# Attention by head pairs: logits on the two row halves, value sums feature-major on the two column halves

## The chip, the core and the metric

The kernel runs on one core of a Trainium2 chip. Time is device microseconds of one execution on that core. Its engines work through their own queues in order and meet at semaphores: PE multiplies matrices into PSUM (eight banks of 128 partitions x 512 floats), DVE and ACT do elementwise work and empty PSUM, POOL does some elementwise work, SP issues the loads.

## What is computed

The reference is two blocks of a network for 256 tokens of 1024 features: feed-forward halves, a Mamba-2 mixer, a sliding-window attention, a mixer of latent attention and RWKV-7, and a layer of experts. The change touches the sliding-window attention of the first block. It has 16 query heads of 64 features, two shared key/value heads (eight query heads each), a window of 128 tokens, a position bias and a sink for each head:

```python
q = rmsnorm((u @ w_q).reshape(bsz, t, ATT_KV_HEADS, ATT_GROUP, ATT_HEAD_DIM), q_norm)
s = jnp.einsum('bqkrd,bskd->bkrqs', qk, kk).astype(jnp.float32) * scale + bias
s = jnp.where(valid, s, -jnp.inf)
m = jnp.maximum(jnp.max(s, axis=-1, keepdims=True), sink)
p = jnp.exp(s - m)
denom = jnp.sum(p, axis=-1, keepdims=True) + jnp.exp(sink - m)
o = jnp.einsum('bkrqs,bskd->bqkrd', (p / denom).astype(vk.dtype), vk)
h = h + o.reshape(bsz, t, ATT_HEADS * ATT_HEAD_DIM) @ w_o
```

## The kernel before

Activations lie feature-major: `h` is 128 partitions x 8 groups of features x 256 tokens. Large products are made of three matmuls on a high and a low part of both operands (`mm3`, L151; `xhi`, `xlo`, `whi`, `wlo`). Weights come in loads of 512 KB (L127), are split by ACT (`whi`, L93) and DVE (`wlo`, L99), and each such piece feeds eight `mm3`, 24 matmuls of 256 columns.

`attention` (L651) is woven from generators: at each `yield` the next one writes its instructions, and what is written first stands first in each engine's queue. Three run in turn: `project(0)`, then `fill` with `project(1..3)` and the output projection, and `heads`. `project(m)` computes q for four heads (L672), copies it to `qT` (L673), squares it on POOL (L675), sums the squares with four matmuls of two columns (L682) and makes the scales `sc` on DVE (L688 to L691). `heads` starts one head at each step.

A head (`attn_head`, L611) takes these steps: logits, queries x keys, from 64 rows of `qT` and `kd` (even heads in the upper half, odd ones in the lower), in two matmuls for tokens 0 to 127 (128 keys) and 128 to 255 (256 keys), L617 and L618; scale and bias, the negated maximum, the bound by the sink on DVE (L621, L622, L624); the exponentials with their sums `den` on ACT (L627); three transposes on PE (L631); their copy `asT` by ACT (L636); the value sums with the transposed weights as the stationary operand and 64 value columns moving, tokens on the partitions, into the banks `po`, which eight heads share (L638 to L640). A float32 matmul stands in the trace as two records, one for each pass; a transpose, and a matmul of `mm3`, as one.

After eight heads `tail` (L708) adds the sink's exponential to `den`, takes the reciprocal, multiplies `po` by it into `otok` (L716), transposes that to feature-major on PE (L724) and splits it to `ohi` (ACT, L727) and `olo` (DVE, L728). Then `proj_half` (L252) of the output projection runs on these four groups of features; the second eight heads feed the second half. `attn_head` is also called by the latent attention of the second block, which stays as it is.

`bcast` (L196) spreads a column over partitions: the column, repeated, is the stationary operand and the identity moves.

Of the kernel before, what the change touches and what calls it, by code (L numbers as in the profile page):

```python
# [17 lines left out]
T = 256  # L18
# [5 lines left out]
def weave(gens, lag=1):  # L24

    live, t = [], 0
    gens = list(gens)
    while gens or live:
        if gens and t % lag == 0:
            live.append(gens.pop(0))  # L30
        for g in list(live):
            if next(g, live) is live:
                live.remove(g)
        t += 1
        yield
# [13 lines left out]
class Ctx:  # L49
# [146 lines left out]
    def bcast(self, rt, st, c, n, out):  # L196

        self.nc.tensor.matmul(out, rt[:, st, c:c + 1].to_broadcast([128, n]), self.ident, start=True, stop=True)
# [452 lines left out]
def attention(K, h, P, kv, w_q, w_o, bias, pool):  # L651
# [11 lines left out]
    otok = pool.tile([128, 2, 1024], F32, name="otok")  # L663
# [30 lines left out]
    def head(hd):  # L694
        kvh, p0, c = hd // 8, 64 * (hd % 2), (hd % 8) * 64
        while hd // 4 not in scaled:
            yield
        if hd % 8 == 0:
            po[kvh] = [K.bank("po") for _ in range(2)]
        s = pool.tile([128, 384], F32, name="as", tag="as", bufs=4)  # L700
        sT = pool.tile([128, 384], F32, name="asT", tag="asT", bufs=3)
        yield from attn_head(K, s, qT[p0:p0 + 64, hd // 2], kd[p0:p0 + 64, kvh], vtok[:, :, kvh * 64:kvh * 64 + 64],
                             sc[:, hd], (bias[:, hd, 128:256], bias[:, hd]), nsink[:, hd:hd + 1], nm[:, hd], den[:, hd],
                             [p[:, c:c + 64] for p in po[kvh]], sT, hd % 4 < 0)
        if hd % 8 == 7:
            tails.append(tail(kvh))

    def tail(g):  # L708
        gs = slice(8 * g, 8 * g + 8)
        V.tensor_tensor(u[:, gs], nm[:, gs], nsink[:, gs].unsqueeze(2).to_broadcast([128, 8, 2]), OP.subtract)  # L710
        A.activation(u[:, gs], u[:, gs], AF.Exp)
        yield
        V.tensor_add(den[:, gs], den[:, gs], u[:, gs])
        V.reciprocal(den[:, gs], den[:, gs])
        for st in range(2):
            V.tensor_tensor(otok[:, st, g * 512:(g + 1) * 512].rearrange("p (a b) -> p a b", b=64),  # L716
                            po[g][st].rearrange("p (a b) -> p a b", b=64),
                            den[:, gs, st].unsqueeze(2).to_broadcast([128, 8, 64]), OP.mult)
        for _ in range(1):
            yield  # L720
        for st in range(2):
            ps = K.bank()
            for i in range(4):
                TE.transpose(ps[:, i * 128:(i + 1) * 128], otok[:, st, (4 * g + i) * 128:(4 * g + i + 1) * 128], K.ident)  # L724
            dst = (slice(None), slice(g * 4, g * 4 + 4), slice(st * 128, st * 128 + 128))
            pr = ps.rearrange("p (a b) -> p a b", b=128)
            A.activation(ohi[dst], pr, AF.Copy)  # L727
            V.tensor_sub(olo[dst], pr, ohi[dst].bitcast(F32))  # L728
            yield
        done.append(g)  # L730

    def heads():
        for _ in weave((head(hd) for hd in range(16)), 1):
            if tails and next(tails[0], tails) is tails:
                tails.pop(0)
            yield
        while tails:
            if next(tails[0], tails) is tails:
                tails.pop(0)
            yield  # L740
# [10 lines left out]
    scaled, tails, done, po = [], [], [], {}  # L751
# [4 lines left out]
    run((p0, 1), (fill(), 1), (heads(), 1))  # L756
# [1213 lines left out]
```

## Time and profile before

| | us |
|---|---|
| median of 3 runs | 2186.6 (2182.05 to 2188.41) |
| profiled execution | 2188.62 |
| its span, first to last instruction | 2186.8 |
| PE busy | 2109.8 (96% of the span) |
| DVE busy | 1584.8 (72%) |
| ACT busy | 1055.1 (48%) |
| POOL busy | 407.1 (19%) |

The page gives for each engine how long it had an instruction at work. Since matmuls overlap, PE can be busy without being at its peak, and the same matmul takes about twice as long where the chip grants the engine its lower clock, 1.2 GHz, in place of 2.4; the granted clock stands in the tables by stretch of time, as a share of the higher one. The rows for the attention, at about 839 to 926 us of the span, follow behind the change.

### The profile page before, as it was taken

The numbers are of one execution on the slowest core, as the hardware profiler recorded it, in microseconds if no ns is written. First come the engines' busy times: TensorE is split into PE (matmuls) and PEld (weight loads), VectorE is DVE, ScalarE is ACT, GpSimd is POOL, SyncE is SP. The second block draws the span as 40 slices with busy tenths as digits, with TensorE's granted clock in tenths as the row PEclk, the third lists the DMA queues.
The fourth block names the chain that finished last, engine by engine and source line by source line (L and its number), as shares of the span: only waits on it lengthen the run. The fifth ranks groups of instructions, "written<-read, shape, count | busy, mean of one in ns | idle before, by whom it ended". The sixth has DMA issues, their size and how long they took to land. (4 is left out here: it accounts for less than half of the span.)

```text
span 2186.8 us, 40880 instructions
## 1 busy us (share of the span) xinstructions
PE 2109.8 (96%) x16474; PEld 1986.3 (91%) x16474; DVE 1584.8 (72%) x2857; ACT 1055.1 (48%) x1770; POOL 407.1 (19%) x310
## 2 busy tenths in 40 slices
PE   8999898899999999999998998999999999999999
PEld 8999887799999998899997878999999998888887
DVE  7665979766567656676659678998788887555655
ACT  5444467444444445454443345553444444454454
POOL 2003335700110021100144315762000000000000
PEclk9999999999999999799998899999999999999999
DMA  6555442377555553245542205542444444555554
GB/s 218 190 185 177 136 135 101 134 191 204 185 181 184 183 184 107 102 169 188 188 164 76 80 30 194 177 151 97 157 162 155 159 160 164 189 188 191 192 188 150
DMA packets 98280, 348.14 MB, mean 159 GB/s; under 512 B 11083, under 2 KB 13996, under 8 KB 97836
## 3 DMA queue, kind: packets, MB, share of 16 engines
q1 hardware_dynamic: 98092, 345.54, 46.6%
q8 instruction: 129, 2.11, 0.4%
q14 instruction: 59, 0.48, 0.1%
HBM read 344.05 MB, written 1.44 MB: 158 GB/s over the span
## 5 line engine op out<-in xcount | busy, mean ns | idle before, releaser
L99 DVE TENSOR_TENSOR wlo<-wraw,whi 128x1024 fp32r<-128x1024 f32 x561 | 701.7, 1252 | 293.9 <-ACT whi L93 292.0
L93 ACT ACTIVATE whi<-wraw 128x1024 fp32r<-128x1024 f32 x644 | 676.5, 1053 | 394.0 <-PE ps L155 198.8
L153 PE MATMUL ps<-xhi,wlo 128*128 128x256 f32 x1960 | 562.7, 287 | 20.4 <-DVE wlo L99 9.6
L154 PE MATMUL ps<-xlo,whi 128*128 128x256 f32 x1960 | 557.3, 284 | 3.2 <-DVE xlo L182 2.6
L155 PE MATMUL ps<-xhi,whi 128*128 128x256 f32 x1960 | 554.9, 283 | 0.0
L153 PEld LDWEIGHTS ps<-xhi,wlo 128*128 128x128 f32 x1960 | 376.2, 192 | 28.8 <-DVE wlo L99 8.6
L154 PEld LDWEIGHTS ps<-xlo,whi 128*128 128x128 f32 x1960 | 376.1, 192 | 5.8 <-DVE xlo L182 5.4
L155 PEld LDWEIGHTS ps<-xhi,whi 128*128 128x128 f32 x1960 | 375.5, 192 | 0.2
L153 PE MATMUL ps<-phi,wlo 128*128 128x256 f32 x1024 | 293.9, 288 | 11.3 <-DVE wlo L99 4.6
L154 PE MATMUL ps<-plo,whi 128*128 128x256 f32 x1024 | 288.1, 281 | 0.0
L155 PE MATMUL ps<-phi,whi 128*128 128x256 f32 x1024 | 287.2, 281 | 0.0
L99 POOL TENSOR_TENSOR wlo<-wraw,whi 128x1024 fp32r<-128x1024 f32 (+1 forms) x83 | 206.8, 2495 | 167.5 <-ACT whi L93 145.5
L153 PEld LDWEIGHTS ps<-phi,wlo 128*128 128x128 f32 x1024 | 193.8, 190 | 13.1 <-DVE wlo L99 5.3
L1676 PE MATMUL pacc<-whi,cl 128*128 128x512 f32 x512 | 203.6, 398 | 1.5 <-DVE cl L1668 1.5
L1678 PE MATMUL pacc<-whi,ch 128*128 128x512 f32 x512 | 200.5, 392 | 0.0
L1677 PE MATMUL pacc<-wlo,ch 128*128 128x512 f32 x512 | 199.2, 389 | 0.0
L153 PE MATMUL ps<-ghi,wlo 128*128 128x256 f32 x704 | 197.9, 281 | 0.0
L154 PE MATMUL ps<-glo,whi 128*128 128x256 f32 x704 | 197.6, 281 | 0.0
L155 PE MATMUL ps<-ghi,whi 128*128 128x256 f32 x704 | 197.5, 280 | 0.0
L154 PEld LDWEIGHTS ps<-plo,whi 128*128 128x128 f32 x1024 | 194.0, 189 | 0.0
L155 PEld LDWEIGHTS ps<-phi,whi 128*128 128x128 f32 x1024 | 193.3, 189 | 0.0
L154 PEld LDWEIGHTS ps<-glo,whi 128*128 128x128 f32 x704 | 132.6, 188 | 0.0
(534 smaller groups left out, 3371.3 us busy)
## 6 DMA issues: line engine op xcount, KB each, us to landing
wraw<-in_w SPq DMA_DIRECT2D x262, 512.0 KB, 3.7
wraw<-in_p_u SPq DMA_DIRECT2D x128, 512.0 KB, 3.6
wraw<-in_p_v SPq DMA_DIRECT2D x128, 512.0 KB, 3.6
wraw<-in_m_win SPq DMA_DIRECT2D x40, 512.0 KB, 3.7
wraw<-in_x_win SPq DMA_DIRECT2D x20, 512.0 KB, 3.6
wraw<-in_m_wout SPq DMA_DIRECT2D x16, 512.0 KB, 3.7
wraw<-in_p_wpq SPq DMA_DIRECT2D x16, 512.0 KB, 4.3
wraw<-in_a_wq SPq DMA_DIRECT2D x8, 512.0 KB, 3.5
```

The source lines that it names most:

```text
L93: nc.scalar.activation(hi, w, AF.Copy)
L99: (nc.vector if lo_eng == "dve" else nc.gpsimd).tensor_sub(lo, w, hi.bitcast(F32))
L153: nc.tensor.matmul(ps, wl, xh, start=first, stop=False)
L154: nc.tensor.matmul(ps, wh, xl, start=False, stop=False)
L155: nc.tensor.matmul(ps, wh, xh, start=False, stop=last)
L1676: TE.matmul(o, cl[:, t], vh[:, f], start=False, stop=False)
L1677: TE.matmul(o, ch[:, t], vl[:, f], start=False, stop=False)
L1678: TE.matmul(o, ch[:, t], vh[:, f], start=False, stop=last)
```

## The change

Heads are computed in pairs: `pair(n)` for heads 2n and 2n+1, eight pairs, a new one every second step, in place of 16 heads at one per step.

- The logits of both heads are written in turn, first the two 128-column matmuls, then the two of 256 columns; one head uses the upper 64 rows and the other the lower, each has its own bank. Ahead of them stands one `K.warm` matmul of 256 columns of zeros into the first of the two banks.
- Scale and bias stay one operation for each head and token half. The maximum is taken for both heads in one operation per token half, the bound by the sink in one for the pair.
- The sink's exponential, its addition to `den` and the reciprocal are done per pair, before the value sums, instead of once per eight heads.
- Of the copies of the transposes, ACT makes the first head's and DVE the second's.
- The value sums have the values (64 columns) as the stationary operand and the transposed weights moving, 256 and 128 columns. Their result is feature-major, one head in the upper 64 partitions of a bank and the other in the lower: on the two column halves.
- Since the tokens now lie along the free dimension, the reciprocals are spread over 64 partitions for each head and token half with `bcast`, four matmuls into the other half of the same bank. ACT copies them (`ao`), DVE multiplies by the value sums, and ACT and DVE split the product into `ohi` and `olo`.
- `otok`, its 16 transposes and `tail` are gone. The first half of the output projection may start after four pairs.

```diff
     def bcast(self, rt, st, c, n, out):
 
-        self.nc.tensor.matmul(out, rt[:, st, c:c + 1].to_broadcast([128, n]), self.ident, start=True, stop=True)
+        r = rt if st is None else rt[:, st]
+        self.nc.tensor.matmul(out, r[:, c:c + 1].to_broadcast([128, n]), self.ident, start=True, stop=True)
...
+    def pair(n):
+
+        kvh, gs, halves = n // 4, slice(2 * n, 2 * n + 2), (slice(0, 64), slice(64, 128))
+        while n // 2 not in scaled:
+            yield
+        s = pool.tile([128, 2, 384], F32, name="as", tag="as", bufs=3)
+        sT = pool.tile([128, 2, 384], F32, name="asT", tag="asT", bufs=2)
+        pl = [K.bank() for _ in range(2)]
+        K.warm(pl[0], 1)
+        for e, p in enumerate(halves):
+            TE.matmul(pl[e][:, 0:128], qT[p, n, 0:128], kd[p, kvh, 0:128], start=True, stop=True)
+        for e, p in enumerate(halves):
+            TE.matmul(pl[e][:, 128:384], qT[p, n, 128:256], kd[p, kvh], start=True, stop=True)
+        yield
+        for e in range(2):
+            hd = 2 * n + e
+            for st, (a, b) in enumerate(SPANS):
+                V.scalar_tensor_tensor(s[:, e, a:b], pl[e][:, a:b], sc[:, hd, st:st + 1], bias[:, hd, 128 - 128 * st:], OP.mult, OP.add)
+        for st, (a, b) in enumerate(SPANS):
+            V.tensor_reduce(nm[:, gs, st], s[:, :, a:b], AX.X, OP.max, negate=True)
+        V.tensor_tensor(nm[:, gs], nm[:, gs], nsink[:, gs].unsqueeze(2).to_broadcast([128, 2, 2]), OP.min)
+        yield
+        for e in range(2):
+            hd = 2 * n + e
+            for st, (a, b) in enumerate(SPANS):
+                A.activation(s[:, e, a:b], s[:, e, a:b], AF.Exp, bias=nm[:, hd, st:st + 1], accum_out=den[:, hd, st:st + 1])
+        V.tensor_tensor(u[:, gs], nm[:, gs], nsink[:, gs].unsqueeze(2).to_broadcast([128, 2, 2]), OP.subtract)
         A.activation(u[:, gs], u[:, gs], AF.Exp)
         yield
+        pt = [K.bank() for _ in range(2)]
+        for e in range(2):
+            for b in range(3):
+                TE.transpose(pt[e][:, b * 128:(b + 1) * 128], s[:, e, b * 128:(b + 1) * 128], K.ident)
         V.tensor_add(den[:, gs], den[:, gs], u[:, gs])
         V.reciprocal(den[:, gs], den[:, gs])
+        yield
+        A.activation(sT[:, 0], pt[0][:, :384], AF.Copy)
+        V.tensor_copy(sT[:, 1], pt[1][:, :384])
+        yield
+        po = K.bank()
+        v = vtok[:, :, kvh * 64:kvh * 64 + 64]
+        for e, p in enumerate(halves):
+            TE.matmul(po[p, 0:256], v[:, 0], sT[:, e, 0:256], start=True, stop=False)
+        for e, p in enumerate(halves):
+            TE.matmul(po[p, 128:256], v[:, 1], sT[:, e, 256:384], start=False, stop=True)
         for st in range(2):
...
+            for e, p in enumerate(halves):
+                K.bcast(den[:, 2 * n + e], None, st, 64, po[p, 256 + st * 128:384 + st * 128])
+        yield
+        o = pool.tile([128, T], F32, name="ao", tag="ao", bufs=2)
+        A.activation(o, po[:, 256:512], AF.Copy)
+        V.tensor_tensor(o, o, po[:, 0:256], OP.mult)
+        yield
+        A.activation(ohi[:, n], o, AF.Copy)
+        V.tensor_sub(olo[:, n], o, ohi[:, n].bitcast(F32))
+        if n % 4 == 3:
+            done.append(n // 4)
...
-    run((p0, 1), (fill(), 1), (heads(), 1))
+    run((p0, 1), (fill(), 1), (weave((pair(n) for n in range(8)), 2), 1))
```

PE's queue behind the last matmul of the q projection (`mm3` on `xhi`), before:

```order
L155 MATMUL ps<-xhi,whi 128x256
L638 MATMUL po<-vtok,asT 128x64
L639 MATMUL po<-vtok,asT 128x64
L640 MATMUL po<-vtok,asT 128x64
L631 MATMUL ps<-cst,as 128x128 x3
L617 MATMUL ps<-kd,qT 128x128
L618 MATMUL ps<-kd,qT 128x256
L638 MATMUL po<-vtok,asT 128x64
```

The same place in the changed kernel (L736 and L738 are the value sums, L199 the spreading, L726 the transposes, L77 the `K.warm` matmul, L704 and L706 the logits):

```order
L155 MATMUL ps<-xhi,whi 128x256
L736 MATMUL ps<-asT,vtok 64x256 x2
L738 MATMUL ps<-asT,vtok 64x128 x2
L199 MATMUL ps<-cst,den 64x128 x4
L726 MATMUL ps<-cst,as 128x128 x6
L77 LDWEIGHTS zero
L77 MATMUL ps<-zero 128x256
L704 MATMUL ps<-kd,qT 128x128 x2
L706 MATMUL ps<-kd,qT 128x256 x2
L682 MATMUL ps<-cst,qsq 128x2 x4
```

One group now serves two heads. From here to the first matmul on `ohi` the queue holds nine value sums, eight heads' transposes, seven heads' logits, eight transposes of `otok` and one group L682 before, and three pairs' value sums, three pairs' transposes, two pairs' logits and one group L682 after.

PE's queue where the output projection begins, before, and then in the changed kernel:

```order
L724 MATMUL ps<-cst,otok 128x128 x4
L638 MATMUL po<-vtok,asT 128x64
L639 MATMUL po<-vtok,asT 128x64
L640 MATMUL po<-vtok,asT 128x64
L631 MATMUL ps<-cst,as 128x128 x3
L153 MATMUL ps<-ohi,wlo 128x256
```

```order
L736 MATMUL ps<-asT,vtok 64x256
L726 MATMUL ps<-cst,as 128x128 x3
L736 MATMUL ps<-asT,vtok 64x256
L738 MATMUL ps<-asT,vtok 64x128 x2
L199 MATMUL ps<-cst,den 64x128 x4
L726 MATMUL ps<-cst,as 128x128 x3
L153 MATMUL ps<-ohi,wlo 128x256
```

Before, the value sums of 13 heads stand ahead of the first matmul on `ohi`; after, those of five pairs. The other pairs' groups stand between the pieces of the output projection, and 120 of its 192 matmuls behind the last of them (108 before).

DVE's queue in the same stretch, before (L728 makes `olo` of the first eight heads):

```order
L621 SCALAR_TENSOR_TENSOR as<-ps,qsc,t5b 128x128
L621 SCALAR_TENSOR_TENSOR as<-ps,qsc,t5b 128x256
L622 TENSOR_REDUCE nm<-as 128x1 x2
L621 SCALAR_TENSOR_TENSOR as<-ps,qsc,t5b 128x128
L624 TENSOR_SCALAR nm<-nm,nsink 128x2
L622 TENSOR_REDUCE nm<-as 128x1
L621 SCALAR_TENSOR_TENSOR as<-ps,qsc,t5b 128x256
L728 TENSOR_TENSOR olo<-ps,ohi 128x4x128
```

and in the changed kernel (L711 scale and bias and L713, L714 the maximum of pair 4, L745 the product of pair 2, L731 the copy of pair 3's second head):

```order
L711 SCALAR_TENSOR_TENSOR as<-ps,qsc,t5b 128x128
L711 SCALAR_TENSOR_TENSOR as<-ps,qsc,t5b 128x256
L711 SCALAR_TENSOR_TENSOR as<-ps,qsc,t5b 128x128
L711 SCALAR_TENSOR_TENSOR as<-ps,qsc,t5b 128x256
L713 TENSOR_REDUCE nm<-as 128x2 x2
L745 TENSOR_TENSOR ao<-ao,ps 128x256
L714 TENSOR_TENSOR nm<-nm,nsink 128x4
L731 COPY asT<-ps 128x384
L720 TENSOR_TENSOR qu<-nm,nsink 128x4
L748 TENSOR_TENSOR olo<-ao,ohi 128x256
```

The copy for which a pair's value sums on PE wait stands behind the logits of the next pair and the product of the one before.

## Rows read from the trace of the kernel before

**Rows 1.** Busy time by engine in stretches cut where the granted clock changes.

```profile
core 0: us, PE busy (x) PEld busy (x) DVE busy (x) ACT busy (x) POOL busy (x), PEclk, DMA share, GB/s
...
844.10:847.60 3.50, 3.50 (x19) 3.28 (x17) 3.50 (x16) 1.35 (x6) 0.00 (x0) 0.51 0.01 2
...
857.80:864.60 6.80, 6.80 (x30) 5.86 (x29) 2.98 (x12) 2.24 (x9) 0.00 (x0) 0.50 0.15 53
...
874.60:902.20 27.60, 27.17 (x107) 21.81 (x108) 12.93 (x47) 9.85 (x36) 0.00 (x0) 0.51 0.06 19
...
sum 87.10, PE 86.38 PEld 76.11 DVE 54.81 ACT 41.69 POOL 9.50; mean PE 12.34 PEld 10.87 DVE 7.83 ACT 5.96 POOL 1.36
```

**Rows 2.** Instructions on `ohi`: count, ns, first and last start.

```profile
L155 PE MATMUL ps<-ohi,whi x64: 276/281/415, 900.1 to 926.4; 128*128 128x256 f32 x64
```

**Rows 3.** Timeline of PE, full clock: start, length, instructions, count.

```profile
870.26 0.50 PE L631 MATMUL ps<-cst,as 128*128 128x128 f32 x3
870.68 0.49 PE L617 MATMUL ps<-kd,qT 64*128 64x128 f32 x2
...
871.53 0.43 PE L638 MATMUL po<-vtok,asT 128*128 128x64 f32 x2
...
872.25 0.50 PE L631 MATMUL ps<-cst,as 128*128 128x128 f32 x3
...
873.53 1.05 PE L682 MATMUL ps<-cst,qsq 128*128 128x2 f32 x8
```

**Rows 4.** Timeline of PE, one head at the lower clock.

```profile
881.41 0.69 PE L638 MATMUL po<-vtok,asT 128*128 128x64 f32 x2
...
885.10 0.69 PE L638 MATMUL po<-vtok,asT 128*128 128x64 f32 x2
```

**Rows 5.** Timeline of PE, long matmuls at the full clock.

```profile
902.82 0.28 PE L153 MATMUL ps<-ohi,wlo 128*128 128x256 f32 x1
902.94 0.28 PE L154 MATMUL ps<-olo,whi 128*128 128x256 f32 x1
```

**Rows 6.** Timeline of PE, the first heads' logits.

```profile
839.34 0.50 PE L617 MATMUL ps<-kd,qT 64*128 64x128 f32 x4
839.66 0.61 PE L618 MATMUL ps<-kd,qT 64*128 64x256 f32 x4
840.10 0.38 PE L617 MATMUL ps<-kd,qT 64*128 64x128 f32 x2
...
841.21 1.05 PE L682 MATMUL ps<-cst,qsq 128*128 128x2 f32 x8 [0.30 <-POOL qsq L675]
```

**Rows 7.** Timeline of PE, two heads' sums in the mamba stage.

```profile
317.37 0.66 PE L490 MATMUL ps<-sc,xtok 128*64 128x256 f32 x4
317.85 0.40 PE L491 MATMUL ps<-sc,xtok 128*64 128x128 f32 x4
318.17 0.50 PE L473 MATMUL ps<-ahl,identr 64*128 64x256 f32 x2
```

**Rows 8.** Timeline of DVE, logits and maxima.

```profile
842.06 0.73 DVE L621 SCALAR_TENSOR_TENSOR as<-ps,qsc,t5b 128x256 f32<-128x256 f32 x2
842.71 0.60 DVE L622 TENSOR_REDUCE nm<-as 128x1 f32<-128x256 f32 x2
843.23 0.22 DVE L624 TENSOR_SCALAR nm<-nm,nsink 128x2 f32<-128x2 f32 x1
```

**Rows 9.** Groups by line, 826 to 927 us: count, busy us, mean ns.

```profile
L99 DVE TENSOR_TENSOR wlo<-wraw,whi 128x1024 fp32r<-128x1024 f32 x16 | 19.7, 1230 | 8.1 <-ACT whi L93 8.1
...
L636 ACT ACTIVATE asT<-ps 128x384 f32<-128x384 f32 x16 | 7.6, 491 | 20.8 <-PE ps L631 19.3 <-PE po L640 1.4
...
L716 DVE TENSOR_TENSOR otok<-po,den 128x512 f32<-128x512 f32 x4 | 2.6, 683 | 0.0
...
L171 DVE SCALAR_TENSOR_TENSOR rsq32t<-rsq32a,rsq32t 128x8 f32<-128x8 f32 x4 | 0.6, 156 | 0.0
```

**Rows 10.** Waits, 826 to 927 us: total us, times, longest.

```profile
DVE TC L792 <- DMA px<-in_xcols: 0.3, 1, 0.3
```

More of the change, by code (lines that the diff above doesn't have):

```diff
@@ L662, in attention @@
     u = pool.tile([128, 16, 2], F32, name="qu")
-    otok = pool.tile([128, 2, 1024], F32, name="otok")
     ohi = pool.tile([128, 8, T], F32R, name="ohi")
@@ L692, in project @@
         scaled.append(m)
-    def head(hd):
-        kvh, p0, c = hd // 8, 64 * (hd % 2), (hd % 8) * 64
-        while hd // 4 not in scaled:
+    def pair(n):
+        kvh, gs, halves = n // 4, slice(2 * n, 2 * n + 2), (slice(0, 64), slice(64, 128))
+        while n // 2 not in scaled:
             yield
[L698 to L706, printed above, removed]
@@ L708, in tail @@
-    def tail(g):
-        gs = slice(8 * g, 8 * g + 8)
-        V.tensor_tensor(u[:, gs], nm[:, gs], nsink[:, gs].unsqueeze(2).to_broadcast([128, 8, 2]), OP.subtract)
+        s = pool.tile([128, 2, 384], F32, name="as", tag="as", bufs=3)
[4 more added lines that the diff above has]
+            TE.matmul(pl[e][:, 0:128], qT[p, n, 0:128], kd[p, kvh, 0:128], start=True, stop=True)
@@ L712, in tail @@
         yield
+        pt = [K.bank() for _ in range(2)]
+        for e in range(2):
+            for b in range(3):
+                TE.transpose(pt[e][:, b * 128:(b + 1) * 128], s[:, e, b * 128:(b + 1) * 128], K.ident)
         V.tensor_add(den[:, gs], den[:, gs], u[:, gs])
         V.reciprocal(den[:, gs], den[:, gs])
-        for st in range(2):
-            V.tensor_tensor(otok[:, st, g * 512:(g + 1) * 512].rearrange("p (a b) -> p a b", b=64),
-                            po[g][st].rearrange("p (a b) -> p a b", b=64),
-                            den[:, gs, st].unsqueeze(2).to_broadcast([128, 8, 64]), OP.mult)
@@ L719, in tail @@
[L719 to L740, printed above, removed]
+        yield
[4 more added lines that the diff above has]
+        v = vtok[:, :, kvh * 64:kvh * 64 + 64]
@@ L749, in fill @@
             yield from K.proj_half(blk, g, ohi[:, 4 * g:4 * g + 4], olo[:, 4 * g:4 * g + 4], h)
-    scaled, tails, done, po = [], [], [], {}
+    scaled, done = [], []
     p0 = project(0)
```

## The prediction, written before the changed kernel ran

> **What bounds the kernel now.** I read the page first: PE has work in nearly the whole span, DVE and ACT in far less of it, so a stage is worth what PE spends in it. The change touches the attention alone, so I then read its stretch, from the first logit matmul to the last matmul on `ohi` at 926.4 us [rows 1, 2]: 87.1 us, of which PE is busy 86.38, DVE 54.81 and ACT 41.69. The windows are cut where the granted clock changes: it is at its lower level (1.2 of 2.4 GHz) in 3.5, 6.8 and 27.6 us, together 37.9 us [rows 1]. Before a fall PE ran heads and narrow `L682` matmuls (at 841.21 and at 873.53 us [rows 3, 6]), and before each rise the long matmuls of a projection. The third stretch has no such matmuls until the output projection begins, and there DVE is busy only 12.93 of 27.6 us. PE sets the pace, at the lower clock.
>
> One head costs PE 1.99 us at the full clock, from one group of transposes to the next: 0.42 for them, 0.85 for the logits, 0.72 for the value sums [rows 3]. At the lower clock it costs 3.69 us [rows 4], 1.85 times as much. So the 37.9 us would be 20.5 at the full clock: the low clock costs 17.4 us. A check: 288 long matmuls (96 of the q projection after the first logits, 192 of the output projection) at 0.12 us [rows 5] are 34.6, three groups `L682` at 1.0 [rows 6] are 3.0, 16 heads are 31.8, and 16 transposes of `otok` at about 0.11 are 1.8; with the 17.4 that makes 88.6, against 87.1 measured.
>
> **The change, part by part: PE.** All at the full clock, for one pair. Logits: the first two heads of before already lie on the two row halves one behind the other, and their eight passes (x4 and x4) take from 839.34 to 840.10, 0.76 us [rows 6], where one head alone takes 0.85. So two heads side by side are shown, and I take 0.9 with the change of mode. Six transposes with the change of mode: 0.84. The filler matmul `K.warm`: one of 256 columns, 0.12. Value sums: the mamba stage has the same pattern (two heads, 64 columns each, 256 and then 128 moving columns, on two column halves of one bank), and it takes from 317.37 to 318.17, 0.80 us [rows 7], against 1.44 for two heads now. The reciprocals' spreading is new: four matmuls of 128 columns on the same halves, as two steps like the `L491` step of 0.32, with one drain less: 0.55, between 0.4 and 0.65. Sum 3.2 us per pair, 25.7 for eight. Now it is 31.8 + 1.8 = 33.6. **PE: -7.9 us.**
>
> **DVE and ACT.** Two logit operations follow each other by 0.65 us for one head, its two maxima by 0.52 [rows 8]. Per pair: 1.3 for the four logit operations, 0.95 for two wider maxima with the same elements, about 0.6 for four small ones, 0.5 for the copy of the second head's transposes (ACT's copy of 384 columns takes 0.491 [rows 9]), and 0.75 for product and difference of 256 columns, which are half of the 0.683 row [rows 9] each and some fixed time. That is 4.1 us. PE needs only 3.2. While projections run between the heads this is covered, because a piece of 24 long matmuls costs PE 2.8 us [rows 5] and DVE one split of weights, 1.23 [rows 9]. Between the last matmul of the q projection and the first of the output projection it is not. By the order PE has there three value sums, three groups of transposes, two of logits and one `L682`, about 3 x 3.2 + 1.0 = 10.6 us; DVE has 3 x 4.1, two splits of weights at 1.23 and 13 small steps for the scales at about 0.16 [rows 9], 16.9 us. The value sums of a pair wait for the copy `L731`, and before it stand four logit operations, two maxima and the product of other pairs; behind it stand the next pair's logits, for which ACT waits, and then the transposes. The difference is 6.3 us if DVE comes in without a lead, and 0 if it is a whole pair ahead. DVE has some lead, since nothing holds it in the projections. **New waits: +5 us**, from 0 to 7.
>
> Here a rule of the Trainium skill speaks against the change. TensorEngine Tiling (Array Packing), Performance Considerations, PSUM Bottleneck, says that tiling speeds up TensorE but not the emptying of PSUM, which may become the bottleneck. This trace agrees in the sums: the pair falls on PE, and rises on DVE. If it held in the whole stretch, it would be the first rival below.
>
> ACT exchanges like for like: its exponentials stay, one copy of `asT` per pair moves to DVE, a copy of the spread sums and smaller pieces of `ohi` come in. The exponential of the sink now stands once per pair instead of once per eight heads, and waits for DVE; behind it is the split of weights, `whi`, which the output projection needs 24 matmuls later. ACT is busy in under half of the stretch [rows 1], and I cost it at nothing; without that cover it would be some 0.2 us per pair, like a small step on DVE. The GpSimd work is the same. On SP the load of `px` goes one weight load later. DVE waits 0.3 us for it now [rows 10]; the last 120 matmuls of the output projection, 14 us of PE, lie over a wait of one or two microseconds.
>
> **The clock.** The three places with an `L682` stay, and after each I expect a fall. What differs is how soon long matmuls follow: before, nine value sums, eight groups of transposes and seven of logits stand between the projections; now three, three and two. I take the first two falls as they are, 3.5 and 6.8 us [rows 1], and for the third the 10.6 us of PE less what passes before the fall, with waits: about 9. So 19.3 us at the lower clock, and as each costs 0.46 of its time, 8.9 us in place of 17.4. **Clock: -8.5 us**, from 0 (as long as now) to -17.4 (no fall at all).
>
> **Sum:** -7.9 + 5 - 8.5 = -11.4 us. The profiled execution took 2188.62 us with a span of 2186.8, so 1.8 lie around it and stay: 2177.2 for one like it. It stands 2.0 above the median of the runs, 2186.6, so against the median I say **2175 us**.
>
> **Rivals.**
> DVE sets the pace and the clock stays low as long as now: -7.9 + 6.3 + 0, 2185 us. For it speaks that the waits thin out PE's work exactly where the clock falls now. Against it: long matmuls come earlier, and each of the first two low stretches ended within about one piece of them [rows 1]. Chance 0.20.
> The clock hardly falls: side by side two heads fill more of PE's time, and with the filler matmul only one short fall remains: -7.9 + 4 - 14, 2169 us. For it: the mamba stage's pairs. Against it: `L682` leaves PE thin whatever the heads do. Chance 0.17.
> Slower: the waits for DVE bring the clock down early, and pieces of 24 long matmuls between heads no longer bring it back, until the last 120. Of 48 us of PE work before those (25.7 + 3.0 + 168 x 0.12) about 70% would be at the lower clock, 34 x 0.85 = 29 us of cost against 17.4 now; -7.9 + 5 + 11.6 is +8.7, 2195 us. The time is longer than before once more than 44 us run at the lower clock (0.46 x 44 is the 17.4 of now and the 2.9 left of the gain). Against it: the rises at 847.6 and 864.6 [rows 1], each after one piece of 24. Chance 0.08.
> The halves do not run side by side here: logits, value sums and spreading cost up to twice, +1.7 us a pair, +13.6 in all: -11.4 + 13.6, 2189 us. Rows 6 and 7 speak against it [rows 6, 7]. Chance 0.02.
>
> **How the numbers follow.** The forecast has 0.53, with its own range of -4 to -17 us (2169.5 to 2182.5), from waits of 0 to 7 and clock costs of 5 to 14. Of the cases, a change of over 0.3% (6.6 us, about what a measurement of this kernel can tell from none) faster holds 0.47 of the forecast, all of the second rival and 0.03 of the first: 0.67. Slower by that much: 0.09, the third rival and a tail of the fourth. Within: 0.24. The range for 8 in 10 goes from 2166 (second rival with fewer waits) to 2187 (first rival and a little).
>
> **What would show it.** In the changed trace: the two heads' logit matmuls start within hundredths of a microsecond of each other, and a pair's group takes about 0.9 us; value sums and spreading about 1.35. PE's waits should be on DVE's copy `L731` and on ACT's exponentials, 5 us in all, and lie after the last q projection. The windows at the lower clock should sum to 15 to 23 us, the output projection should begin 10 to 15 us earlier than at 899.7, and the last 120 matmuls should run unbroken. I would be wrong if the low clock still lasts over 30 us, if PE waits over 8 us for DVE, or if time changes outside 839 to 927 us by more than 2 or 3 us (the granted clock could fall elsewhere as stages shift).

## The result and the profile after

The changed kernel takes 2166.2 us (median of 12 executions) where the kernel before took 2187.9 beside it: a ratio of 0.991, 95% interval 0.989 to 0.9931, about 20 us less (21.7 between the medians). The direction was as forecast; the size was not, since the sum gave 11.4 us. The one of the twelve that was profiled ran at a granted clock of 0.555 from end to end (3338.5 us), so the rows below are from another execution.

> The changed kernel as it is, for a profile at the usual clock. The measured gain is about 20 us where 11.4 were forecast (-7.9 PE work, +5 waits for DVE, -8.5 clock). Theory: PE's work fell as forecast, but the stretch at the lower clock is shorter than the 19 us forecast, 5 us or less, and the waits for DVE are under 5 us. Rival 1: the clock falls as forecast, about 19 us, and the waits are absent. Rival 2: the attention gains only some 11 us, and the rest comes from other stages, whose spans shift by 5 us or more.

That one took 2160.96 us, beside 2183.33 for the kernel before. The kernel before was profiled once more as well, to see how regular its low clock is.

> The kernel before once more, for a second profile of it. Theory: the fall of the clock in its attention is regular, 30 to 40 us at the lower level, 85 to 88 us from the first logits to the last matmul of the output projection. Rival: it differs from execution to execution, under 25 us here, and then part of the 17.4 us that I put on the low clock belongs to the one execution that was profiled.

It took 2191.68 us. The first theory held for this execution: 37.5 us at the lower level in 87.3 us of attention, in three stretches as before [rows 1]. It does not hold for all. Of the 80 executions of the kernel before that stand beside the runs below, ten took 2169.9 to 2174.4 us at a mean granted clock of 0.978 to 0.982, and the other 70 took 2179.0 to 2199.5 us at 0.966 to 0.979; both profiles are of the larger group. So one profile in which the clock stays up does not by itself show that an edit holds it, and the clocks of all executions of a kernel are named below where it matters. Busy time by engine in stretches of time, the kernel before again (columns as in rows 1):

```profile
core 0: us, PE busy (x) PEld busy (x) DVE busy (x) ACT busy (x) POOL busy (x), PEclk, DMA share, GB/s
...
847.30:850.70 3.40, 3.40 (x17) 3.20 (x16) 3.40 (x16) 1.30 (x6) 0.00 (x0) 0.50 0.01 2
860.90:867.70 6.80, 6.80 (x29) 5.85 (x28) 2.98 (x12) 2.24 (x9) 0.00 (x0) 0.50 0.14 53
878.00:905.30 27.30, 26.87 (x106) 21.52 (x105) 12.69 (x46) 9.60 (x34) 0.00 (x0) 0.50 0.06 20
842.50:929.80 87.30, 86.58 (x539) 76.34 (x539) 55.03 (x162) 41.94 (x108) 9.75 (x10) 0.78 0.25 90
```

The same view of the changed kernel, cut at the start of the output projection, answers rows 1 and 2:

```profile
843.20:875.80 32.60, 32.60 (x298) 27.14 (x298) 30.98 (x113) 24.17 (x77) 3.12 (x3) 1.00 0.24 82
875.80:907.00 31.20, 30.11 (x265) 27.83 (x264) 26.27 (x58) 17.55 (x41) 6.54 (x7) 1.00 0.48 164
843.20:907.00 63.80, 62.71 (x561) 54.97 (x561) 57.25 (x171) 41.71 (x117) 9.66 (x10) 1.00 0.36 123
```

The attention takes 63.8 us instead of 87.3, and PEclk reads 1.00: in this execution the clock doesn't fall in it at all. PE is busy for all but 1.1 us, and its waits there come to one line (total us, times, longest):

```profile
PE ps L726 <- ACT as L719: 1.1, 2, 0.9
```

The rest of the execution took 2160.96 - 63.8 = 2097.2 us; it was 2101.5 in the first profile of before and 2104.4 in the second. In the profiles of the experiments below that leave those stages as they are it lies between 2097.0 and 2104.4. So some 7 us outside the attention differ from execution to execution of the same code, and what is said below of parts of the change goes by the attention's own stretch, with the medians beside it.

One pair on PE at the full clock, which answers rows 3 and 6 (start, length, instructions, count):

```profile
870.25 0.65 PE L736 MATMUL ps<-asT,vtok 128*64 128x256 f32 x4
870.74 0.39 PE L738 MATMUL ps<-asT,vtok 128*64 128x128 f32 x4
870.95 0.61 PE L199 MATMUL ps<-cst,den 128*64 128x128 f32 x8
871.49 0.87 PE L726 MATMUL ps<-cst,as 128*128 128x128 f32 x6
872.20 0.27 PE L77 MATMUL ps<-zero 128*128 128x256 bf16 x1
872.40 0.49 PE L704 MATMUL ps<-kd,qT 64*128 64x128 f32 x4
872.73 0.60 PE L706 MATMUL ps<-kd,qT 64*128 64x256 f32 x4
873.26 0.43 PE L736 MATMUL ps<-asT,vtok 128*64 128x256 f32 x1
```

From start to start: value sums 0.70, spreading 0.54, transposes 0.71, filler 0.20, logits 0.86, together 3.01 us for two heads.

### The profile page after: what moved, and what is told of

Read it like the earlier page. It is cut to its first block, busy times and chain, and to the rows that moved or that the text cites. A ratio compares the mean times of both kernels' runs of the same rounds, so it can differ in the third digit from the quotient of the medians.

```text
span 3336.8 us, 40935 instructions
## 1 busy us (share of the span) xinstructions
PE 3312.4 (99%) x16498; PEld 2977.1 (89%) x16498; DVE 1574.6 (47%) x2867; ACT 1067.6 (32%) x1780; POOL 395.1 (12%) x310
## 4 chain that ended last, share of the span: by engine, by line
PE 99%; DVE 1%; ACT 0%; issue 0%; DMA 0%; SPq 0%; DVEq 0%; ACTq 0%
PE ps L153 23%; PE ps L155 23%; PE ps L154 23%; PE pacc L1688 6%; PE pacc L1686 6%; PE pacc L1687 6%; PE ps L1633 2%; PE wo L153 1%; PE wo L155 1%; PE wo L154 1%; PE ps L199 1%; PE ps L491 0%; PE ps L1557 0%; PE ps L726 0%; PE ps L77 0%; PE ps L190 0%
## 5 line engine op out<-in xcount | busy, mean ns | idle before, releaser
L153 PE MATMUL ps<-xhi,wlo 128*128 128x256 f32 x1960 | 750.6, 383 | 7.3 <-DVE wlo L124 7.2
L154 PE MATMUL ps<-xlo,whi 128*128 128x256 f32 x1960 | 747.1, 381 | 0.4 <-DVE xlo L182 0.2
L155 PE MATMUL ps<-xhi,whi 128*128 128x256 f32 x1960 | 747.1, 381 | 0.0
L153 PEld LDWEIGHTS ps<-xhi,wlo 128*128 128x128 f32 x1960 | 574.2, 293 | 15.0 <-DVE wlo L124 7.4
L155 PEld LDWEIGHTS ps<-xhi,whi 128*128 128x128 f32 x1960 | 578.2, 295 | 0.8 <-issue 0.2
L154 PEld LDWEIGHTS ps<-xlo,whi 128*128 128x128 f32 x1960 | 576.5, 294 | 1.7 <-DVE xlo L182 1.2
L153 PE MATMUL ps<-phi,wlo 128*128 128x256 f32 x1024 | 395.5, 387 | 2.4 <-ACT phi L1507 2.4
L155 PE MATMUL ps<-phi,whi 128*128 128x256 f32 x1024 | 392.4, 383 | 0.0
L154 PE MATMUL ps<-plo,whi 128*128 128x256 f32 x1024 | 390.6, 381 | 0.9 <-DVE plo L1508 0.9
L155 PEld LDWEIGHTS ps<-phi,whi 128*128 128x128 f32 x1024 | 294.6, 288 | 0.0
L155 PE MATMUL ps<-ghi,whi 128*128 128x256 f32 x704 | 269.8, 383 | 0.0
L155 PEld LDWEIGHTS ps<-ghi,whi 128*128 128x128 f32 x704 | 208.3, 296 | 0.0
```

The costliest lines, as they stand in the source:

```text
L153: nc.tensor.matmul(ps, wl, xh, start=first, stop=False)
L154: nc.tensor.matmul(ps, wh, xl, start=False, stop=False)
L155: nc.tensor.matmul(ps, wh, xh, start=False, stop=last)
```

## The experiments: which part keeps the clock up

The largest difference to the forecast is the clock, so four kernels take the change apart. The kernel without the filler:

```diff
-        K.warm(pl[0], 1)
```

> The changed kernel without the filler matmul ahead of each pair's logits; all else is as changed. What is asked of the four runs of this call: which part of the change keeps the granted clock at its full level in the attention (0 us at the lower level there, against 37.9 before). Theory, sums: the new form of the value sums does it (64 stationary columns and 256 or 128 moving ones, where 128 stationary ones met 64 moving). Then the clock stays up without the filler, under 4 us at the lower level in the attention, and the time is the changed kernel's less eight fillers at about 0.12 us: 0 to 1 us below it, some 20 to 22 us below before. Rival, filler: the filler does it; then 15 to 30 us at the lower level come back, which cost 7 to 14 us, and the kernel is only 8 to 14 us below before.

Measured 2162.05 us, ratio to before 0.990 (0.9867 to 0.9933), the same as the changed kernel within the interval. Its attention by engine (here and below the columns are those of rows 1, and rows at a PEclk of about 0.50 are all that fell):

```profile
843.90:907.20 63.30, 61.92 (x555) 54.44 (x555) 57.15 (x172) 41.84 (x117) 9.61 (x10) 1.00 0.36 123
```

The clock stays up without the filler, with a mean over the whole execution of 0.978 to 0.985 in all eight, and the attention is 0.5 us shorter: the theory held. The filler alone, in the kernel before (logits of every second head):

```diff
     ps = K.bank()
+    K.warm(ps, fillers)
     TE.matmul(ps[:, 0:128], q[:, 0:128], k[:, 0:128], start=True, stop=True)
```

> The kernel before with nothing added but eight fillers in the attention, one ahead of the logits of every second head. Theory, sums: the clock falls as before, 30 to 40 us at the lower level between the first logits and the end of the output projection, and the time is before's plus about 1 us (8 x 0.12). Rival, filler: the low level there shrinks to under 10 us, which gives back 13 to 17 us of the 17.4 that it costs, and the time is 12 to 16 us below before.

Measured 2182.6, ratio 0.9989 (0.9958 to 1.002).

```profile
859.60:869.80 10.20, 10.20 (x45) 9.22 (x45) 4.78 (x22) 2.72 (x10) 0.00 (x0) 0.50 0.03 8
844.60:922.40 77.80, 76.66 (x546) 67.31 (x546) 54.71 (x161) 41.74 (x108) 9.63 (x10) 0.93 0.29 101
```

Neither theory has this right. In the profiled execution, with eight fillers, 10.2 us are at the lower level instead of 37.5, and the attention takes 77.8 us. The medians show only 4 us of these 9.5, the interval reaches to no change at all, and the ten executions go from 2168.6 us at a mean clock of 0.983 to 2191.0 at 0.972. So how much the fillers hold by themselves is not shown. The first part of the change with the filler, but the old value sums and tails:

```diff
-        po = K.bank()
-        for e, p in enumerate(halves):
-            TE.matmul(po[p, 0:256], v[:, 0], sT[:, e, 0:256], start=True, stop=False)
+        for e in range(2):
+            TE.matmul(p0, sT[:, e, 0:128], v[:, 0], start=True, stop=True)
+            TE.matmul(p1, sT[:, e, 128:256], v[:, 0], start=True, stop=False)
+            TE.matmul(p1, sT[:, e, 256:384], v[:, 1], start=False, stop=True)
```

> The first part of the change and the filler alone: logits of two heads in turn on the two row halves, by pairs, but value sums token by token with 64 moving columns, the division and the 16 transposes per eight heads as before. Theory, sums: the clock still falls, 20 to 38 us at the lower level, since the old value sums are there; PE saves 8 x (2 x 0.85 - 0.9) = 6.4 us on the logits and pays 1 for fillers, so 4 to 12 us below before (12 if the low stretches get shorter by a third). Rival, logits or filler: the clock stays up, under 8 us at the lower level, and the time is 19 to 23 us below before (6.4 - 1 and 14 to 17 of clock).

Measured 2169.4, ratio 0.993 (0.9898 to 0.9961).

```profile
858.80:862.20 3.40, 3.40 (x18) 3.40 (x18) 2.34 (x9) 1.38 (x6) 0.00 (x0) 0.50 0.22 67
882.70:889.50 6.80, 4.95 (x22) 4.56 (x23) 4.28 (x12) 3.90 (x16) 0.00 (x0) 0.50 0.00 0
843.60:914.90 71.30, 68.24 (x545) 63.39 (x545) 56.45 (x145) 38.48 (x100) 9.69 (x10) 0.93 0.31 110
```

As in the profile with the filler alone, 10.2 us remain at the lower level. That is between the two theories, and so is the time, 17 us below before; 1.85 us of the second stretch are PE's own idle time. The second part alone, heads one by one and no filler:

```diff
-    TE.matmul(o[0], sT[:, 0:128], v[:, 0], start=True, stop=True)
+        for e, p in enumerate(halves):
+            TE.matmul(po[p, 0:256], v[:, 0], sT[:, e, 0:256], start=True, stop=False)
+        for e, p in enumerate(halves):
+            TE.matmul(po[p, 128:256], v[:, 1], sT[:, e, 256:384], start=False, stop=True)
+        yield
+        for st in range(2):
+            for e, p in enumerate(halves):
+                K.bcast(den[:, 2 * n + e], None, st, 64, po[p, 256 + st * 128:384 + st * 128])
```

> The second part alone: logits of one head after the other as before, no filler, but value sums feature-major on the two column halves with the reciprocals spread, once per two heads. Theory, sums: the clock stays up, under 8 us at the lower level in the attention. PE pays 1.35 us per pair for sums and spreading where 1.44 stood, and the 16 transposes (1.8 us) go: -2.5 us of PE and -14 to -17 of clock, 15 to 20 us below before, if waits add little. Rival, logits or filler: 25 us or more at the lower level remain, and the time is 0 to 6 us below before.

Measured 2172.4, ratio 0.9939 (0.9916 to 0.9962).

```profile
842.70:913.50 70.80, 70.50 (x555) 58.15 (x555) 59.51 (x196) 42.36 (x118) 10.17 (x10) 1.00 0.32 112
```

No time at the lower level: the second part alone does it. It saves 16.5 us of attention, and 14 by the medians, near the 15 to 20 of the first theory, though PE's work is not the 2.5 us less that I expected (below). The second part has three things in it, the form of the value sums, the spreading, and the tails that go (the odd heads' copy is on DVE too, as in the change). Without the spreading, on top of the last kernel, so that the division is left out:

```diff
-                K.bcast(den[:, 2 * n + e], None, st, 64, po[p, 256 + st * 128:384 + st * 128])
-        A.activation(o, po[:, 256:512], AF.Copy)
+        A.activation(o, po[:, 0:256], AF.Copy)
```

> The kernel of e4_sums_only (heads one by one, no filler, feature-major value sums) without the spreading of the reciprocals: the division by the sums of the exponentials is left out, and the value sums are multiplied by themselves in its place, so that DVE and ACT do as much as before. Eight times 0.54 us of PE go (the pair's four spreading matmuls in the changed kernel's trace), 4.3 us. Question: of the second part, which keeps the clock up, the value sums' form or the added spreading matmuls? Theory, form: 0 to 4 us at the lower level in the attention, which then takes 66 to 68 us (70.8 in e4_sums_only), and the time is 3 to 5 us below e4_sums_only's 2172.4. Rival, spreading: 15 us or more at the lower level come back, the attention takes 73 us or more, and the time is 3 us or more above e4_sums_only's.

Measured 2172.4, ratio 0.9938 (0.9911 to 0.9965).

```profile
881.20:884.60 3.40, 3.40 (x18) 2.99 (x18) 3.40 (x16) 2.64 (x11) 0.00 (x0) 0.50 0.00 0
840.90:909.40 68.50, 66.20 (x491) 55.67 (x491) 59.62 (x196) 41.70 (x117) 9.40 (x10) 0.98 0.32 113
```

3.4 us fall, at the first matmuls of the output projection, so the spreading has a small part in it at most. Of the 4.3 us that PE loses the attention gains 2.3; PE idles 2.3 us here, 0.3 in the kernel with the spreading. The median shows no gain. The transposes of the tails, from the other side, taken out of the kernel before, so that the sums stay token-major:

```diff
-            ps = K.bank()
-            for i in range(4):
-                TE.transpose(ps[:, i * 128:(i + 1) * 128], otok[:, st, (4 * g + i) * 128:(4 * g + i + 1) * 128], K.ident)
+            ps = otok[:, st, g * 512:(g + 1) * 512]
```

> The kernel before without the 16 transposes of otok in its tails: ohi and olo are taken from otok as it stands, so the transposing of the sums is left out. PE loses 16 transposes of about 0.11 us, 1.8 us, at the lower clock 3.4 (two groups of four take 0.86 each there, 724 in the trace). Theory (the value sums' form): the low stretch stays, 28 to 37 us in the attention, and the time is 2 to 6 us below before. Rival, the tails: the second part of the change kept the clock up because it took the tails away; then under 12 us at the lower level remain and the time is 13 us or more below before.

Measured 2185.5, ratio 0.9993 (0.9971 to 1.0016). The profile shows 17.1 us at the lower level (two stretches of 6.8 and 10.2) in 77.1 us, between the two theories; but it is of an execution of 2174.2 us, the fastest of ten, of which eight took 2185 to 2189. The two executions that were 10 us faster, this one and one of 2176.3 us, have a mean granted clock of 0.980, the other eight 0.971 to 0.976: they differ by the clock, as the executions of before do, and the profile is not of the usual case. By the median these transposes matter little, as the first theory said.

What is left is the form of the value sums, and that was tested by itself. The old ones move 64 columns for each load of 128 x 128 transposed exponentials [rows 3]. In the kernel before each of these matmuls, but for those of the last head of each eight, was made to move its columns twice, work that nothing needs:

```diff
+    if twice:
+        v0, v1 = (x.unsqueeze(1).to_broadcast([128, 2, 64]) for x in (v0, v1))
+        o = [x.rearrange("p (a b) -> p a b", b=64) for x in o]
```

> The kernel before with one edit: in the attention each matmul of the token-major value sums moves its 64 value columns twice (128 moving columns; the second copy lands where the next head's sums overwrite it), for all heads but the last of each eight. Nothing else moves or changes. In the trace of before one such matmul follows the other after 0.22 us at the full clock, and the logit matmuls of 128 columns after 0.21 to 0.22, so 128 columns should cost PE little more than 64: 0 to 0.05 us each, 0 to 2 us for 42 of them. Theory (what brings the clock down are value sums that move few columns for each weight load): with more work and nothing gained the lower level in the attention shrinks from 37.5 us to under 10, and the time falls by 8 to 16 us. Rival (it is the order, the tail or the time until the output projection): 30 us or more remain at the lower level, and the time is before's or 1 to 4 us more.

Measured 2172.8, ratio 0.9932 (0.9901 to 0.9963): 14.3 us below before by the medians, for more work. Its attention by engine:

```profile
840.40:911.80 71.40, 70.64 (x539) 62.88 (x539) 54.84 (x162) 41.61 (x108) 9.64 (x10) 1.00 0.31 110
```

Its timeline of PE, the value sums of the eighth head, which keeps 64 columns, and of a later one with 128, both behind logits:

```profile
873.01 0.43 PE L642 MATMUL po<-vtok,asT 128*128 128x64 f32 x2
873.28 0.39 PE L643 MATMUL po<-vtok,asT 128*128 128x64 f32 x2
873.50 0.39 PE L644 MATMUL po<-vtok,asT 128*128 128x64 f32 x2
873.73 0.28 PE L631 MATMUL ps<-cst,as 128*128 128x128 f32 x1
...
877.00 0.49 PE L642 MATMUL po<-vtok,asT 128*128 128x128 f32 x2
877.33 0.39 PE L643 MATMUL po<-vtok,asT 128*128 128x128 f32 x2
877.55 0.39 PE L644 MATMUL po<-vtok,asT 128*128 128x128 f32 x2
877.77 0.39 PE L642 MATMUL po<-vtok,asT 128*128 128x128 f32 x2
```

The clock does not fall once in this attention. Over the whole execution its mean is 0.979 to 0.983 in all seven; 11 of the 80 executions of before come to 0.979. Three matmuls of 64 columns take 0.72 us (873.01 to 873.73), as before the change [rows 3], and of 128 columns 0.77 (877.00 to 877.77): twice the columns for 0.05 us a head. The order of the work, the tails and the three `L682` groups are those of before. So the number of columns that the value sums move matters here, and widening them is enough to hold the clock. What it is about narrow sums that brings the clock down no run shows, and they are not the only way to keep it up: the paired logits with the filler left 10.2 us with the old sums. This kernel also gives what the clock was worth without a factor taken from rows: the old arrangement at the full clock takes at most 71.4 us, 15.9 less than 87.3 (these are two profiles; by the medians it is 14.3).

The Trainium skill, in TensorE: Matmul & The Clock Gate, section HAM oscillation — how this bites in real kernels, puts a falling clock down to stretches in which the engine idles. The attention of before does not agree: PE was busy 86.58 of 87.30 us there, and the clock fell for 37.5.

## The experiments: halves, DVE, and a further use

What lying side by side is worth, with every matmul on the whole array and one head after the other:

```diff
-            TE.matmul(pl[e][:, 0:128], qT[p, n, 0:128], kd[p, kvh, 0:128], start=True, stop=True)
+            TE.matmul(pl[e][:, 0:128], qT[:, n, 0:128], kd[:, kvh, 0:128], start=True, stop=True)
-            TE.matmul(po[p, 0:256], v[:, 0], sT[:, e, 0:256], start=True, stop=False)
+            TE.matmul(po[:, 0:256], vtok[:, 0], sT[:, e, 0:256], start=True, stop=False)
```

> The changed kernel with nothing side by side: logits of the two heads one after the other over all 128 rows (so each head's logits are the sum over both heads), value sums and spreading over all 128 columns (the two key-value heads' values at once, so both halves hold the second head's result). The number of matmuls and their columns are the changed kernel's. Per pair PE should pay at the full clock 2 x 384 columns in four passes, 1.28 us and some 0.2 of drains, for logits (0.86 now) and again for value sums (0.70 now), and about 0.95 for spreading (0.54 now): 1.7 more, 13 to 14 us for eight. Theory (the form of the value sums keeps the clock up, with or without halves): 0 to 4 us at the lower level, attention of about 77 us, time 11 to 14 us above the changed kernel. Rival, side by side keeps the clock up: 15 us or more at the lower level, attention of 84 us or more, time 19 us or more above. Rival, the pace is not PE's: under 7 us above.

Measured 2170.2, ratio 0.9927 (0.9901 to 0.9952).

Busy time by engine, and then the timeline of PE:

```profile
841.80:912.70 70.90, 70.90 (x562) 68.98 (x562) 58.39 (x171) 41.29 (x117) 9.58 (x10) 1.00 0.31 110
```

```profile
868.25 0.59 PE L734 MATMUL ps<-asT,vtok 128*128 128x256 f32 x2
...
869.55 1.06 PE L199 MATMUL ps<-cst,den 128*128 128x128 f32 x8
870.45 0.82 PE L725 MATMUL ps<-cst,as 128*128 128x128 f32 x6
```

Value sums take 1.30 us a pair (868.25 to 869.55) instead of 0.70, spreading 0.90 instead of 0.54. The attention is 7.1 us longer than the changed kernel's, not 13, partly because PE no longer waits (0 us idle). The clock stays up without halves, so it is not the lying side by side that holds it (the filler is still there; the widened kernel has neither). And with nothing side by side the kernel is still some 16 us below before: of the 23.5 us that the attention gains in the profiles, about a third is the halves and two thirds the clock (by the medians the halves are 4 of 21.7).

Whether DVE was near its limit, as the forecast had it, with both copies of the transposes there:

```diff
-        A.activation(sT[:, 0], pt[0][:, :384], AF.Copy)
+        V.tensor_copy(sT[:, 0], pt[0][:, :384])
```

> The changed kernel with both copies of a pair's transposed exponentials on DVE: eight more copies of 0.55 us there, 4.4 us, and eight of 0.49 fewer on ACT. My prediction held that DVE would make PE wait 5 us; the changed kernel's attention shows PE idle for only 1.1 us of 63.9. Theory, DVE has a lead of a pair: PE's idle time grows by under 1.5 us and the time stays within 2 us of the changed kernel. Rival, DVE stands just at its limit between the q projection and the output projection (three pairs there): PE idles 2 to 5 us more, and the time is 2 to 5 us above.

Measured 2168.8, ratio 0.9906 (0.9878 to 0.9933), which the times alone do not tell from the changed kernel. The profile does (busy time by engine, then the timeline of PE with the idle time before an instruction and what ended it):

```profile
840.20:907.10 66.90, 63.76 (x562) 55.39 (x562) 59.62 (x179) 38.75 (x110) 8.02 (x8) 1.00 0.33 114
```

```profile
868.59 0.65 PE L736 MATMUL ps<-asT,vtok 128*64 128x256 f32 x2 [1.20 <-DVE asT L730]
...
873.24 0.65 PE L736 MATMUL ps<-asT,vtok 128*64 128x256 f32 x2 [0.85 <-DVE asT L730]
```

PE idles 3.1 us instead of 1.1, on the copies, between the last q projection and the output projection (at 875.83 there): the place and the line that the prediction named. In the changed kernel PE does not wait there at all; its 1.1 us of waits for ACT lie later, and here too. Two of the eight added copies lie in that place, at 0.55 us each, and PE waits 2.05 us for DVE. So the rival in this expectation is right in the profile, DVE stands just short of its limit, though the times don't resolve it. This is the rule on PSUM that the prediction took from the Trainium skill (TensorEngine Tiling (Array Packing), PSUM Bottleneck): it begins to decide with one more copy per pair on DVE, 2.05 us of waits.

Last, the fillers where PE waits in the mamba stage, to see if the clock can be held there too:

```diff
         ps = K.bank()
+        K.warm(ps, 16)
         for st in range(2):
             K.bcast(rt, st, 0, 128, ps[:, st * 128:(st + 1) * 128])
```

> The changed kernel with 16 fillers in each of the four groups of the mamba stage, ahead of the matmuls that spread the group's reciprocal root (L199 there). In the changed kernel's trace PE waits there for DVE's rtn four times, 11.1 us in all (2.4 to 3.3 each), and after each of these waits the clock is at its lower level: 346.2, 373.5, 393.9 (6.8 us each) and 414.4 (3.4), 23.9 us that cost 0.46 of their length, 11 us. The fillers, 16 x 0.11 = 1.7 us, lie within the waits and should cost nothing. Theory, what e2_filler_only showed in the attention holds here: a wait filled with matmuls doesn't bring the clock down. The four stretches go, or shrink to a third, and the time falls by 7 to 11 us below the changed kernel, to 0.986 of before. Rival, these waits are not what brings the clock down, or matmuls of zeros don't count: the stretches stay and the time is the changed kernel's, within 1 us. Rival, the fillers run late and hold up what follows: 2 to 5 us above it.

Measured 2168.8, ratio 0.9934 (0.9911 to 0.9958): no gain over the changed kernel. The waits for `rtn`, first in the changed kernel, then here:

```profile
PE ps L199 <- DVE rtn L176: 11.1, 4, 3.3
```

```profile
PE ps L199 <- DVE rtn L176: 9.7, 4, 4.5
```

and three of the four places here:

```profile
343.70:347.00 3.30, 2.16 (x19) 1.69 (x18) 3.27 (x14) 3.27 (x6) 0.73 (x1) 1.00 0.60 214
373.90:380.70 6.80, 6.80 (x31) 5.66 (x32) 6.80 (x12) 4.14 (x9) 3.90 (x3) 0.50 0.46 155
397.80:404.60 6.80, 5.68 (x26) 4.76 (x27) 4.76 (x13) 1.62 (x4) 1.65 (x3) 0.50 0.23 80
```

Where a wait of about 1.1 us was left behind the fillers (the first place and the last) the clock stayed up; in the other two waits of 2.9 and 4.5 us remained and it fell. That can't be put down to the fillers. The kernel with both copies on DVE has the changed kernel's mamba stage without them; in its profile PE waits 2.56 us at the first place and the clock stays up there too, where in the changed kernel's it fell with a wait of 2.58 us. Over the whole stretch from 317 to 420 us the granted clock reads 0.93 in that profile, 0.93 with the fillers, and 0.88 in the changed kernel's. The fillers took PE 7.8 us (1.96 for each 16), the waits shrank by 1.4, and `rtn` came later: nearer to the third theory. None of these kernels beats the changed one beyond the intervals; without its filler it is as fast.

## Why the prediction was right in direction and short in size

| term | forecast | measured in the attention |
|---|---|---|
| PE work | -7.9 | -7.9 (70.64 busy in the widened kernel, 62.71 after) |
| new waits | +5 | +0.3 (0.76 idle there, 1.09 after) |
| clock | -8.5 | -15.9 (87.3 to 71.4, the widened kernel) |
| sum | -11.4 | -23.5 |

The 87.3 and the 71.4 us are of single profiles; the medians of before and after differ by 21.7 us. That puts 2166.2 us at the low end of the range, because the two terms that were off, waits by 4.7 us and the clock by 7.4, were off the same way. The forecast's own bounds also reach further than the -17 that I gave: no waits and a clock cost of 5 make -20.3.

**PE.** The step held, and by its parts: logits 0.86 forecast 0.9, six transposes 0.71 for 0.84, value sums and spreading 1.24 for 1.35, filler 0.20 for 0.12; 3.01 us a pair for 3.2. Both sums were 0.6 too high, 71.2 for 70.64 before and 34.6 + 3.0 + 25.7 = 63.3 for 62.71 after, so the difference holds. What it is made of was not as I would have told it: the second part alone has PE busy 70.50, as much as the old arrangement at the full clock. The 7.8 us come with the first part, eight pairs whose logits lie side by side and whose transposes stand together.

**Waits.** This step failed. I set 16.9 us of DVE work against 10.6 us of PE work between the last q projection and the output projection. PE's side was 9.5 us (the 10.6 had three groups of logits in it where the order of the queue gives two). DVE was busy 8.87 of them:

```profile
866.30:875.80 9.50, 9.50 (x92) 6.97 (x92) 8.87 (x31) 7.58 (x27) 1.04 (x1) 1.00 0.19 61
```

DVE's rows of that stretch tell what I counted too much:

```profile
865.85 1.39 DVE L711 SCALAR_TENSOR_TENSOR as<-ps,qsc,t5b 128x128 f32<-128x128 f32 x4
...
869.50 1.39 DVE L711 SCALAR_TENSOR_TENSOR as<-ps,qsc,t5b 128x128 f32<-128x128 f32 x4
...
873.50 1.22 DVE L99 TENSOR_TENSOR wlo<-wraw,whi 128x1024 fp32r<-128x1024 f32 x1
876.63 0.53 DVE L731 COPY asT<-ps 128x384 f32<-128x384 f32 x1
878.35 0.74 DVE L711 SCALAR_TENSOR_TENSOR as<-ps,qsc,t5b 128x128 f32<-128x128 f32 x2
```

Two groups of logits lie there and not three, one split of weights and not two; the third copy and the third group of logits come after 875.8, when the output projection has begun and covers them. A pair costs DVE even more than I said, 4.45 us for 4.1 (11.2 of `L711`, 8.2 of `L713`, 6.7 of `L745` and `L748`, 5.1 in four small groups and 4.4 of `L731`, over eight). The mechanism is real, as the doubled copies show, and the lead that I allowed for as the lower end (0) was the case.

**Clock.** This is the term that was mis-sized, and by its cause. I wrote that the three places with an `L682` stay and that after each I expect a fall, with only the length of the third to change. The `L682` groups stand there after the change too (869.27 is one), and no fall follows. What I took as a bystander, the heads' own value sums, was the part that mattered, as the widened kernel shows. That the clock hardly falls was my second rival, with nearly the right time (2169) for a partly wrong reason: it named two heads side by side and the filler, and neither is needed. But little is missing for the clock to hold in the kernel before: in ten of its 80 executions the time and the mean clock are those of the widened kernel.

The forecast's other marks: the two heads' first logit matmuls start 7 ns apart in the trace. The output projection's first `L155` starts at 876.2 instead of 900.1 [rows 2], 23.9 us earlier; counted from the first logits, at 843.2 and 839.3 [rows 6], it is 27.8. Forecast were 10 to 15; all of the low clock went. PE's only waits are the two on ACT's exponentials, so the last matmuls run unbroken. Outside the attention the time moved by more than the 2 or 3 us that I had allowed, 4.3 and 7.2 us against the two profiles of before, with the same spread among kernels that share that code; the granted clock differs there from execution to execution, as in the mamba stage above.

## To carry to other kernels

When PE is busy throughout and the clock still falls, look at the matmuls that move few columns for each load of weights: here 64 columns against 128 x 128, where moving twice as many cost 0.05 us a head and gave 15.9 us back in the stretch. Try that widening before a restructuring, so that a change of order isn't credited with what the clock gives, and look at the mean clock of every execution before one profile is believed. Count the second engine's work by where its instructions stand on its own queue, not by whole pairs.

## What the runs showed of the hardware

A value-sum matmul of 64 moving columns and one of 128 are both followed by the next after 0.22 us (873.28 to 873.50, 877.33 to 877.55). The granted clock fell for 37.5 us in an attention in which PE idled for 0.72 of 87.3 us. The same code with the same wait of PE (2.58 and 2.56 us in the mamba stage) lost the clock in one execution and kept it in another.
